# The head of an S5 stage: lag kernels in 16-row bands, C sums as a third PE term, 128-row transposes, identity matmuls between PE's steps

## The chip, the cores and the metric

The kernel runs on one core of one Trainium2 chip. The metric is the device time of one execution in microseconds (us), the median of several runs.

## The reference, cut to what matters

Input is x of 256 tokens by 1024 channels in fp32. Two blocks of two layers follow each other, eight stages in all: S5 mixer, SwiGLU, stick-breaking attention, SwiGLU, and twice a hybrid layer with its feed-forward part. The change touches the first stage alone, up to its gelu:

```python
bu_re = jnp.einsum('blgh,gph->lbgp', u, bb_re)
bu_im = jnp.einsum('blgh,gph->lbgp', u, bb_im)
_, _, s_re, s_im = lax.associative_scan(
    _ssm_combine, (a_seq_re, a_seq_im, bu_re, bu_im), axis=0)
y = (jnp.einsum('lbgp,ghp->blgh', s_re, c_re.astype(f32))
     - jnp.einsum('lbgp,ghp->blgh', s_im, c_im.astype(f32)))
y = y.reshape(bsz, seq, D_MODEL) + d_skip.astype(f32) * x.astype(f32)
h = jax.nn.gelu(y).astype(x.dtype)
val, gate = jnp.split(h @ w_glu, 2, axis=-1)
```

There are 64 groups of 16 channels, and 64 complex states in each group. The scan is linear with a constant factor (lambda) for each state.

## The kernel before

`s5_states` (from L186) computes that head. The main stream behind it multiplies with w_glu and all later weights; each of its matmuls is three fp32r products, wh by xTh, wh by xTl and wl by xTh (L783 to L785).

The head cuts the 256 tokens into 32 chunks (NC) of 8 tokens (TC). Two groups share the 128 partitions, so there are 32 pairs (NGP), in two halves f of 16. What happens inside a chunk is a table of lag kernels, 8 lags by 16 by 16 for each group; what happens between chunks is a short scan over 32 states. The steps have names, and one string, `ORDER`, sets the order in which they are written for TensorE, ScalarE, GpSimd and VectorE. SyncE's queue, which issues the DMAs, is ordered by the tile framework. The steps that matter here:

- L317 to L320: B and C are transposed in 32-column pieces (L252). Br and Bi are copied by ScalarE, their sum Bs is a GpSimd addition (L319).
- `ug`, `ut`, `us`: ScalarE gathers x into two tiles xTl and xTh (L406). TensorE transposes each in pieces of 32 rows, 64 transposes in all (L412). ScalarE stores u (L416).
- `cp`, `cs`: C times the discretisation factors (L446 to L452), giving cc0, cc1, cc2.
- `vp`, `vt`, `vs`: V, the input side, is B times powers of lambda, 24 VectorE products (L457) that read a table in PSUM (`lt`); 24 times four transposes on TensorE (L487); 24 copies (L491). `sm`, `sd`, `st`, `ss` make the chunk states of it (L500, L504, L509, L519).
- `wp`, `wq`: W, the output side, is C times powers of lambda by the three-product rule for complex numbers. GpSimd makes 24 products (L457 with LR, LRs and LRd); 16 sums (L468) on VectorE, some on GpSimd, combine them into a real and an imaginary half.
- `lp`, `lc`, `ld`: lag kernels. TensorE multiplies B with W (L598), ScalarE copies seven lags into `kz` (L602), VectorE adds the d_skip diagonal to the eighth (L605).
- `lw`: the shift. Eight DMAs for each of 4 quarters c and each half f, 64 in all and 64 KB each, copy windows of `kz` into `lagged` (L609), the band matrix that `tm` multiplies with u (L626). `kz` is one buffer for both halves, so the copies of f=1 overwrite what the DMAs of f=0 read.
- `mg`, `bo`: the scan between chunks on VectorE, up (three merges) and down (six border steps) for each half, four operations per step (L549 to L552).
- `om`: states times W into the same PSUM tiles (L633). `os` stores them (L638), `ot` transposes them back in pieces of 32 rows (L645), `og` is the gelu (L649), `oh` and `ol` split into the fp32r halves xTh and xTl (L652, L655).
- `wd`, `wh`, `wl` load and split the first w_glu tile early (L674 to L682); `hd` loads x again for the residual.

The main stream's weight loads (L737) use the pool `raws` with four buffers, and stand behind the shift DMAs in SyncE's queue.

Of the kernel before, what the change touches and what calls it, by code (L numbers as in the profile page):

```python
# [19 lines left out]
P = 128  # L20
# [145 lines left out]
ORDER = """
cp10 cp11 cs1 dk vp10 ug1 cp00 ug0 wp01 cp01 wp11 ut3 vp12 ut1 cs2 vt12 us3 ut0 vp01 vs12 cs0 wp21 vp11 wp31 us0 us1
vp02 vt10 vp00 vs10 vt01 vs01 vp31 ut4 vt11 wp22 wp02 wp30 vp30 wp00 ut2 vp22 vt02 vs11 wp20 us2 vt00 vs02 sm1 vt30
wq30 vp32 vs00 wp10 wq01 sm0 us4 vp21 vt22 sd1 vs30 dt wp12 wr1 st1 wq00 vs22 vt32 vp20 wq10 sd0 vt31 vp42 ds st0 vs32
wq11 vs31 ut7 ss0 wp32 wq21 vt20 vt21 wq31 wp70 ss1 vs20 sm3 wp50 dm vs21 wq20 wr0 vp41 sm2 wp40 sd3 sd2 wd vt42 lp0  # L170
bp0 ld01 vs42 vp51 vt41 ut5 lc00 wp71 ld00 lc01 lw00 vp50 wp51 vp52 vt51 wp61 wp42 st2 vs41 vt50 wp52 vp40 wq50 wp60
vs51 wp62 wp41 st3 wp72 lw03 ss2 vt40 vp70 us7 ut6 vs50 vs40 bt0 sm4 vp72 ss3 wq60 vt72 sd4 vp71 vs72 vt52 vs52 wh0
vt70 st4 bp1 vs70 wq51 lw01 vp62 us5 sm5 ss4 vp61 lw02 sd5 us6 vt61 bt1 wh1 vt71 wq70 vs71 vs61 vt62 vp60 wq40 st5
wq61 wq41 ss5 mg00 wq71 vt60 lp1 vs62 mg01 lc10 bp2 lc11 ld10 sm7 ld11 vs60 mg02 sd7 sm6 st7 wl1 bp3 bo00 sd6 ss7 bo01
bo02 st6 bo03 ss6 bo04 mg10 bo05 mg11 mg12 bo10 bo11 bo12 tm0 om0 os01 os00 bo13 lw13 lw10 ot1 ot2 og1 lw11 bo14 og2
oh11 ol11 ot3 oh21 ot0 lw12 ol21 oh10 og0 oh01 bo15 oh20 tm1 ol10 ol01 og3 om1 oh30 oh00 ol20 os11 wl0 os10 ot4 oh31
og4 oh40 ot7 ot6 hd ol00 og7 oh41 ol31 ol30 oh71 og6 ol40 oh70 ol41 ol70 oh61 ot5 og5 oh60 ol71 ol61 ol60 oh51 ol51
oh50 ol50
# [3 lines left out]
def s5_states(nc, tc, a, V, S, G, T, const, raws, ats, hpool, mm_ps, tp_ps, xts, ident, load_h, **_):  # L182
# [5 lines left out]
    nsm, nv = [0], [0]  # L188
# [22 lines left out]
    with tc.manual_schedule(engines=PAP):  # L211
# [103 lines left out]
        Br, Bi, Bs = (z.tile([P, NGP + (n != "Bs"), SH], F32, name=n) for n in ("Br", "Bi", "Bs"))  # L315
# [44 lines left out]
        squares, powers_at = [], []  # L360
# [32 lines left out]
        def ycol(ch):  # L393
            return first(("gel", ch), lambda: buf("gel", [P, SEQ]))
# [25 lines left out]
        for i in range(NK):  # L420
            step(f"ut{i}", u_transpose, i)
            step(f"us{i}", u_store, i)


        dsk, mask32, dmask = sm([P, 2, 8], "dsk"), sm([P, 32], "mask32"), sm([P, 2, 8, SH], "dmask")

        def skip_transpose():
            pd = tl["pd"] = tp_ps([P, 2 * 8])
            for c in range(4):
                T.matmul(pd[32 * c:32 * c + 32], d4[:, c, :], ident[:16, :16], start=True, stop=True)  # L430

        def skip_blocks():
            sh = [P, 2, 8, SH]
            G.tensor_mul(dmask, mask32[:, :SH].unsqueeze(1).unsqueeze(1).to_broadcast(sh), dsk.unsqueeze(3).to_broadcast(sh))

        step("dt", skip_transpose)
        step("ds", lambda: S.copy(dsk.rearrange("p f g -> p (f g)"), tl["pd"]))
        step("dk", lambda: V.tensor_reduce(mask32, ident.rearrange("p (c h) -> p h c", h=32), axis=AX.X, op=ALU.add))
# [22 lines left out]

        def w_product(i, k):
            dst = tmp(("wa", i), "wa", [P, 4, TC - 1, SH]) if k == 0 else W(k - 1)[:, 4 * i:4 * i + 4, :TC - 1, :]
            times(G, dst, cc[k], (LRr, LRs, LRd)[k], i, 1, TC - 1)

        def w_sum(i, k):
            w, e = W(k)[:, 4 * i:4 * i + 4, :TC - 1, :], (V, G)[i in POOL_SUMS]
            (e.tensor_add, e.tensor_sub)[k](w, w, tl["wa", i])  # L468

        for k in range(2):  # L470
            step(f"wr{k}", lambda k: S.copy(W(k)[:, :, TC - 1, :], cc[2 - k]), k)
        for i in range(8):
# [48 lines left out]

        def border_power(lv):

            L = sm([P, 3, NGP], f"L{lv}")
            lr, li = L[:, 0], L[:, 2]
            if lv == 0:
                V.tensor_copy(L[:, 0::2], LR[:, 0])
            else:
                pr, pi = squares[-1][:, 0], squares[-1][:, 2]
                V.tensor_mul(x1, pr, pr)  # L530
                V.tensor_mul(d2, pi, pi)
                V.tensor_sub(lr, x1, d2)
                V.scalar_tensor_tensor(li, pr, 2.0, pi, op0=ALU.mult, op1=ALU.mult)
            V.tensor_scalar(L[:, 1], li, -1.0, None, op0=ALU.mult)
            squares.append(L)
            powers_at.append(L)

        def border_table(lv):

            t = lt[1][:, 256 + 96 * lv:352 + 96 * lv].rearrange("p (i g) -> p i g", g=NGP)  # L540
            S.copy(t, powers_at[lv])
            powers_at[lv] = t

        def cmac(dst, x, lv, f, n, plus):
# [9 lines left out]
        def merge(f, lv):  # L554
            gs = slice(16 * f, 16 * f + 16)
            a0 = level(lv)[:, :, gs]
            cmac(level(lv + 1)[:, :, gs, :], a0[..., 0::2], lv, f, NC >> (lv + 1), a0[..., 1::2])

        def border(f, k):

            gs = slice(16 * f, 16 * f + 16)
            s, top = before()[:, :, gs], level(3)[:, :, gs]
            if k == 0:
                V.memset(s[..., 0:1], 0.0)
                V.tensor_copy(s[..., 8:9], top[..., 0:1])
            elif k < 3:
                cmac(s[..., 8 * k + 8:8 * k + 9], s[..., 8 * k:8 * k + 1], 3, f, 1, top[..., k:k + 1])
            else:
                lv = 5 - k
                st = 1 << lv  # L570
                cmac(s[..., st::2 * st], s[..., 0::2 * st], lv, f, NC >> (lv + 1), level(lv)[:, :, gs, 0::2])

        for lv in range(4):
            step(f"bp{lv}", border_power, lv)
        for lv in range(2):
            step(f"bt{lv}", border_table, lv)
        for f in range(2):
            for lv in range(3):
                step(f"mg{f}{lv}", merge, f, lv)
            for k in range(6):  # L580
                step(f"bo{f}{k}", border, f, k)
# [3 lines left out]
        kz = sm([P, 2 * TC - 1, 8, SH], "kz")  # L585
        G.memset(kz[:, TC:], 0.0)

        def by_parity(x, e):
            return x.rearrange("p t (q e) h -> p q e t h", e=2)[:, :, e]

        def lag_products(f):
            ks = tl["ks", f] = [mm_ps([P, 4, TC, SH]) for _ in range(G2)]
            for q in range(4):
                for k in range(2):
                    for c in range(4):
                        for e in range(G2):
                            gp, rows = 4 * (4 * f + c) + q, slice(64 * e, 64 * e + 64)
                            T.matmul(ks[e][32 * c:32 * c + 32, q], (Br, Bi)[k][rows, gp:gp + 2],  # L598
                                     W(k)[rows, gp].rearrange("p t h -> p (t h)"), start=(k == 0), stop=(k == 1))

        def lag_copy(f, e):
# [906 lines left out]
```

## Time and profile before

| what | value |
|---|---|
| median of 3 runs | 1380.1 us (1380.06 to 1381.06) |
| the profiled execution's own time | 1381.14 us |
| its span in the profile | 1379.2 us |
| TensorE busy | 1333.6 us, 97% of the span |
| VectorE busy | 915.7 us, 66% |
| ScalarE busy | 682.9 us, 50% |
| GpSimd busy | 86.3 us, 6% |
| mean granted TensorE clock | 0.986 |
| head, to the first matmul of the next projection (acc) | 129.1 us |

Times in a timeline or a chain are us from the start of the span. A group of equal instructions is one row with its count (x8). A busy time includes the pipeline's drain, so two rows that follow each other can overlap. "PEclk" is the clock that TensorE was granted, as a share of full speed.

### The profile page before, as it was taken

What the parts mean: (1) busy time and instruction counts of PE and PEld (TensorE: products, weight loads), DVE (VectorE), ACT (ScalarE), POOL (GpSimd) and SP (SyncE); (2) the same over time, 40 slices, a digit from 0 to 9 for tenths busy, and PEclk for the clock granted to TensorE, in tenths of its full rate; (3) what the DMA queues carried; (4) which work ended last, traced back from release to release, by engine and by line L of the source; (5) the groups of instructions that cost most, each with busy time, mean ns of one, the idle gap of its engine ahead of it and who ended that gap; (6) DMA issues with size and microseconds to landing.
All of it is one profiled execution on the core that took longest, in us unless ns stands there. A gap on an engine that the chain in (4) does not pass through costs nothing.

```text
span 1379.2 us, 20690 instructions
## 1 busy us (share of the span) xinstructions
PE 1333.6 (97%) x7439; PEld 1102.1 (80%) x7439; DVE 915.7 (66%) x1924; ACT 682.9 (50%) x1065; POOL 86.3 (6%) x153
## 2 busy tenths in 40 slices
PE   6769999999999999999999999999999999999998
PEld 5657878888888878888777888888887788888887
DVE  8677675555776775555888667555568866756462
ACT  3526444444587554444546545444455554545351
POOL 6400000000011100000200000000001000000000
PEclk9869999999999999999999999999999999999999
DMA  4359766556553475565364555564654535556561
GB/s 78 65 122 297 217 193 193 189 185 198 172 176 115 125 228 192 188 187 191 92 192 148 187 171 169 190 213 162 204 169 133 174 123 183 183 184 199 167 207 53
DMA packets 143398, 234.94 MB, mean 170 GB/s; under 512 B 16192, under 2 KB 84864, under 8 KB 143232
## 3 DMA queue, kind: packets, MB, share of 16 engines
q1 hardware_dynamic: 143296, 233.63, 54.5%
q8 instruction: 58, 0.95, 0.3%
q14 instruction: 44, 0.36, 0.1%
HBM read 228.35 MB, written 1.05 MB: 166 GB/s over the span
## 4 chain that ended last, share of the span: by engine, by line
PE 86%; DVE 5%; SPq 3%; DMA 2%; issue 1%; POOL 1%; ACT 1%; ACTq 0%; DVEq 0%; POOLq 0%
PE acc L784 8%; PE acc L785 8%; PE acc L783 8%; PE mm_ffn_g_t L784 5%; PE mm_ffn_g_t L785 5%; PE mm_ffn_g_t L783 5%; PE mm_ff_g_t L783 4%; PE mm_ff_g_t L785 4%; PE mm_ff_g_t L784 4%; SPq L609 3%; PE tp L842 2%; PE mm_hy_t L783 2%; PE mm_hy_t L785 2%; PE mm_hy_t L784 2%; DVE wl L746 1%
## 5 line engine op out<-in xcount | busy, mean ns | idle before, releaser
L746 DVE TENSOR_TENSOR wl<-raw,wh 128x512 fp32r<-128x512 f32 (+1 forms) x834 | 542.8, 686 | 147.2 <-ACT wh L740 136.1
L740 ACT CAST wh<-raw 128x1024 fp32r<-128x1024 f32 (+1 forms) x417 | 436.4, 1048 | 241.7 <-PE mm_ffn_g_t L784 36.5
L783 PE MATMUL acc<-wh,bTh 128*128 128x512 f32 x544 | 213.4, 392 | 0.0
L784 PE MATMUL acc<-wh,bTl 128*128 128x512 f32 x544 | 212.1, 390 | 0.4 <-DVE bTl L829 0.3
L785 PE MATMUL acc<-wl,bTh 128*128 128x512 f32 x544 | 212.3, 390 | 0.0
L783 PE MATMUL mm_ffn_g_t<-wh,xTh 128*128 128x512 f32 x352 | 140.6, 400 | 1.4 <-ACT xTh L828 1.4
L784 PE MATMUL mm_ffn_g_t<-wh,xTl 128*128 128x512 f32 x352 | 137.7, 391 | 0.4 <-DVE xTl L829 0.4
L785 PE MATMUL mm_ffn_g_t<-wl,xTh 128*128 128x512 f32 x352 | 137.6, 391 | 0.0
L829 DVE TENSOR_TENSOR bTl<-tp,bTh 128x256 fp32r<-128x256 f32 (+1 forms) x104 | 52.7, 513 | 124.2 <-ACT bTh L828 124.2
L784 PEld LDWEIGHTS acc<-wh,bTl 128*128 128x128 f32 x544 | 102.2, 188 | 21.9 <-DVE bTl L829 1.1
L828 ACT CAST bTh<-tp 128x256 fp32r<-128x256 f32 (+1 forms) x104 | 45.3, 443 | 149.2 <-PE tp L842 135.5
L785 PEld LDWEIGHTS acc<-wl,bTh 128*128 128x128 f32 x544 | 102.1, 188 | 21.3
L783 PEld LDWEIGHTS acc<-wh,bTh 128*128 128x128 f32 x544 | 102.2, 188 | 21.1 <-ACT bTh L828 0.3
L783 PE MATMUL mm_ff_g_t<-wh,xTh 128*128 128x512 f32 x256 | 102.7, 401 | 0.0
L785 PE MATMUL mm_ff_g_t<-wl,xTh 128*128 128x512 f32 x256 | 100.0, 391 | 0.0
L784 PE MATMUL mm_ff_g_t<-wh,xTl 128*128 128x512 f32 x256 | 99.7, 390 | 0.0
L783 PEld LDWEIGHTS mm_ffn_g_t<-wh,xTh 128*128 128x128 f32 x352 | 66.1, 188 | 14.4 <-ACT xTh L828 1.8
L784 PEld LDWEIGHTS mm_ffn_g_t<-wh,xTl 128*128 128x128 f32 x352 | 66.3, 188 | 13.8 <-DVE xTl L829 1.1
L785 PEld LDWEIGHTS mm_ffn_g_t<-wl,xTh 128*128 128x128 f32 x352 | 66.1, 188 | 13.8
L783 PE MATMUL mm_hy_t<-wh,xTh 128*128 128x512 f32 (+1 forms) x160 | 60.9, 381 | 0.8 <-DVE at L1289 0.6
L784 PE MATMUL mm_hy_t<-wh,xTl 128*128 128x512 f32 (+1 forms) x160 | 59.2, 370 | 1.5 <-DVE xTl L829 1.3
L785 PE MATMUL mm_hy_t<-wl,xTh 128*128 128x512 f32 (+1 forms) x160 | 59.2, 370 | 0.0
(458 smaller groups left out, 2037.2 us busy)
## 6 DMA issues: line engine op xcount, KB each, us to landing
raw<-in_w_ff_dram SPq DMA_DIRECT2D x128, 512.0 KB, 4.6
raw<-in_ffn_w_gu_dram SPq DMA_DIRECT2D x176, 256.0 KB, 4.2
raw<-in_w_in_dram SPq DMA_DIRECT2D x64, 512.0 KB, 4.1
raw<-in_ffn_w_down_dram SPq DMA_DIRECT2D x44, 512.0 KB, 4.6
raw<-in_ssm_w_glu_dram SPq DMA_DIRECT2D x32, 256.0 KB, 4.7
raw<-in_sb_w_qkv_dram SPq DMA_DIRECT2D x32, 256.0 KB, 4.2
raw<-in_w_out_dram SPq DMA_DIRECT2D x16, 512.0 KB, 4.3
raw<-in_ssm_w_out_dram SPq DMA_DIRECT2D x8, 512.0 KB, 5.0
```

The source lines that it names most:

```text
L609: nc.sync.dma_start(out=lagged(f)[SH * j:SH * j + SH, c].rearrange("p t g h -> p (t g h)"), in_=kz[32 * c:32 * c + SH, j:j + TC].rearrange ...
L740: S.copy(wh, raw)
L746: V.tensor_sub(l2[:, sl], r2[:, sl], h2[:, sl])
L783: T.matmul(ps, xh[:, k], wh, start=first, stop=False)
L784: T.matmul(ps, xl[:, k], wh, start=False, stop=False)
L785: T.matmul(ps, xh[:, k], wl, start=False, stop=last)
L828: S.copy(hi, ps)
L829: V.tensor_sub(lo, ps, hi)
L842: T.transpose(pt[:, k, :], src[:, k * P:(k + 1) * P], ident)
```

## The change

It touches the head alone.

- **Shift.** `kz` has 16-row bands, one for each quarter of the groups (n = 0 to 3, at partitions 32n), for both halves at once. Eight DMAs for each n write two quarters c each, 32 in all, and only the lags that are not zero. What stays zero in `lagged` is written before by four DMAs of 1 MB each (`lz`) from the zeroed `kz`.
- **C sums.** The `wq` sums are gone. The LR product stays as a tile `wd`, and TensorE adds it as a third term: in `lp` with Bd = Br - Bi (96 matmuls of a half where 64 stood, and 8 more for the diagonal), in `om` with `gap`, the difference of the states' halves (96 for 64). Bs is made on TensorE with 32 fp32 matmuls by the identity (`both`) and a ScalarE copy.
- **Transposes.** x takes 16 transposes of 128 rows instead of 64, the outputs 16 instead of 64; gelu, high and low halves run on 512 columns at once, 4 each.
- **Scan.** The first border steps run for both halves at once; the later ones apart as before.
- **Identity matmuls.** A name "=N" in `ORDER` writes N matmuls of the identity by 64 columns of it into columns 448 on of the PSUM tile `lt[1]`, whose other columns hold tables that VectorE reads.

```diff
-cp10 cp11 cs1 dk vp10 ug1 cp00 ug0 wp01 cp01 wp11 ut3 vp12 ut1 cs2 vt12 us3 ut0 vp01 vs12 cs0 wp21 vp11 wp31 us0 us1
...
+cp00 cp01 =12 dt ug0 =29 ut0 cp10 vp01 ds cp11 vt01 bm ug1 us00 us01 vp02 wd vs01 ut1 us10 =1 vt02 vp00 dk vp12 vs02
...
-        G.tensor_add(Bs, Br[:, :NGP], Bi[:, :NGP])
         Cc = [transposed(lambda hh: raw[:, hh, :], pv_ps) for raw in c_raw]
+        both = tp_ps([P, SH, NGP])
+        for hh in range(SH):
+            for i, raw in enumerate(b_raw):
+                T.matmul(both[:, hh, :], raw[:, :, hh], i32, start=(i == 0), stop=(i == 1))
+        S.copy(Bs, both.rearrange("p h g -> p g h"))
...
+        def u_transpose(n):
+
+            pu = tl["pu", n] = tp_ps([P, 4, 4, NC])
+            for k in range(4):
+                T.transpose(pu[:, k].rearrange("p r c -> p (r c)"),
+                            tl["xg", n // 2][:, 4 * (n % 2) + k].rearrange("c t h -> c (t h)"), ident)
...
-        def w_sum(i, k):
-            w, e = W(k)[:, 4 * i:4 * i + 4, :TC - 1, :], (V, G)[i in POOL_SUMS]
-            (e.tensor_add, e.tensor_sub)[k](w, w, tl["wa", i])
-
+        def columns(k, rows, gp):
+            return (wd if k == 2 else W(k))[rows, gp].rearrange("p t h -> p (t h)")
+
+        step("bm", lambda: G.tensor_sub(Bd, Br, Bi))
...
+        def lag_zeros(n):
+            nc.sync.dma_start(out=lagged(n // 2)[:, 2 * (n % 2):2 * (n % 2) + 2].rearrange("p c t g h -> p (c t g h)"),
+                              in_=kz.rearrange("p c t g h -> p (c t g h)"))
...
+        def lag_spread(n):
             for j in range(TC):
-                nc.sync.dma_start(out=lagged(f)[SH * j:SH * j + SH, c].rearrange("p t g h -> p (t g h)"),
-                                  in_=kz[32 * c:32 * c + SH, j:j + TC].rearrange("p t g h -> p (t g h)"))
...
+                nc.sync.dma_start(out=lagged(n // 2)[SH * j:SH * j + SH, 2 * (n % 2):2 * (n % 2) + 2, :TC - j].rearrange("p c t g h -> p c (t g h)"),
+                                  in_=kz[32 * n:32 * n + SH, :, j:].rearrange("p c t g h -> p c (t g h)"))
...
+        def state_outputs(f, k):
+            for gi, q, e in places:
+                gp, rows = 16 * f + 4 * q + gi, slice(64 * e, 64 * e + 64)
+                w = columns(k, rows, gp)
+                T.matmul(tl["pc", f][e][32 * q:32 * q + 32, gi, :w.shape[1]],
+                         gap[rows, gp - 16 * f, :] if k == 2 else before()[rows, k, gp, :], w, start=False, stop=(k == 2 and gi == 3))
...
             for name in ORDER.split():
-                steps.pop(name)()
+                if name[0] == "=":
+                    for _ in range(int(name[1:])):
+                        T.matmul(lt[1][:, 448:], ident, ident[:, :64], start=True, stop=True)
+                else:
+                    steps.pop(name)()
```

The order on two engines. TensorE, from the transposes of B and C to the first transposes of V; before:

```order
L252 MATMUL pv<-ident,c_136 128x32 x16
L412 MATMUL tp<-ident,xTl 128x32 x16
L487 MATMUL pv<-ident,v 128x128 x4
L412 MATMUL tp<-ident,xTh 128x32 x8
L487 MATMUL pv<-ident,v 128x128 x8
```

and with the change:

```order
L249 MATMUL pv<-ident,c_136 128x32 x16
L322 MATMUL tp<-ident,big_134 128x32 x32
L728 MATMUL lt_124<-ident 128x64 x12
L434 MATMUL tp<-ident,dpad 64x32 x2
L728 MATMUL lt_124<-ident 128x64 x29
L415 MATMUL tp<-ident,xTh 128x128 x4
L495 MATMUL pv<-ident,v 128x128 x4
L415 MATMUL tp<-ident,xTh 128x128 x4
```

32 matmuls for Bs and 41 identity matmuls (L728) now stand between the transposes of C and the first transposes of x.

TensorE, at the end of the head, with the change (`tp<-ident,raw` are the output transposes, `pv<-big_634` is `tm1`):

```order
L676 MATMUL tp<-ident,raw 128x128 x8
L728 MATMUL lt_124<-ident 128x64 x7
L822 MATMUL mm_s_g_t_1770<-wh,xTh 128x512
L651 MATMUL pv<-big_634,u 32x128 x32
L728 MATMUL lt_124<-ident 128x64
L664 MATMUL pv<-big_587,c_1238 32x128 x32
```

The first matmul of the main stream, which needs the high half of the first outputs, stands ahead of `tm1` and `om1`; before, it stood behind them.

SyncE's queue around the first main weight loads; before:

```order
L609 DMA big_1258<-kz 16x1024 x32
L150 DMA h<-in_x_dram 128x1024 x2
L737 DMA raw<-in_ssm_w_glu_dram 128x2x256 x8
L848 DMA lng<-in_ln_mix_g_dram 128x1024
```

and with the change:

```order
L150 DMA h<-in_x_dram 128x1024 [waits DMAHW4_49,DVE_49]
L150 DMA h<-in_x_dram 128x1024 [waits DMAHW5_49,DVE_49]
L887 DMA lng<-in_ln_mix_g_dram 128x1024 [waits DMAHW2_49,DMAHW1_49,DMAHW3_49,DMAHW0_49,DMAHW6_49,DVE_49,DMAHW7_49,PE_49,Pool_49]
L776 DMA raw<-in_ssm_w_glu_dram 128x2x256 [waits Activation_49]
L776 DMA raw<-in_ssm_w_glu_dram 128x2x256 [waits DVE_49,PE_49,Activation_49]
```

The load of `lng` has moved ahead of all main weight loads. It waits for TensorE (the last `om1` matmul), VectorE, GpSimd and the shift DMAs; the weight loads behind it wait with it, since a queue issues in order.

## Rows read from the trace of the kernel before

**Rows 1.** Windows of two stretches: length, busy (count) by engine, PEclk, DMA share, GB/s.

```profile
33.00:54.00 21.00, 17.95 (x387) 14.68 (x386) 16.82 (x27) 15.12 (x36) 17.60 (x17) 1.00 0.27 46
85.00:99.00 14.00, 9.32 (x224) 8.23 (x224) 6.97 (x18) 3.00 (x11) 0.00 (x0) 0.63 0.58 154
```

**Rows 2.** The chain of waits, 63 to 108 us: start, length, what.

```profile
63.90 2.35 DMA lag<-kz
66.35 0.98 ACT kz L602 x2
...
89.95 2.45 DMA big<-kz
92.44 3.63 PE mm L626 x56
96.07 3.16 PE mm L633 x128
99.25 0.69 DVE raw L638
...
102.01 5.19 DMA raw<-in_ssm_w_glu_dram
```

**Rows 3.** SyncE's queue, timeline: start, length, the issues as one row.

```profile
44.01 21.11 SPq L609 DMA_DIRECT2D lag<-kz  x32
67.61 22.93 SPq L609 DMA_DIRECT2D big<-kz  x32
...
91.69 14.27 SPq L737 DMA_DIRECT2D raw<-in_ssm_w_glu_dram  x8
```

**Rows 4.** TensorE, timeline of the head.

```profile
10.09 3.62 PE L252 MATMUL pv<-ident,c 32*128 32x32 f32 x32
...
23.65 1.97 PE L487 MATMUL pv<-ident,v 128*128 128x128 f32 x8
...
35.47 1.04 PE L487 MATMUL pv<-ident,v 128*128 128x128 f32 x8
36.35 0.38 PE L509 MATMUL mm<-ident,sls 128*128 128x128 f32 x2
...
47.03 1.08 PE L500 MATMUL mm<-vT,u 128*32 128x128 f32 x32
...
108.19 0.59 PE L783 MATMUL mm_s_g_t<-wh,xTh 128*128 128x512 f32 x1
...
129.14 0.39 PE L783 MATMUL acc<-wh,bTh 128*128 128x512 f32 x1
```

**Rows 5.** ScalarE, timeline of the head.

```profile
10.60 1.28 ACT L321 ACT_TABLE_LOAD   x1
...
15.80 0.39 ACT L355 ACTIVATE lt<-LR 128x256 f32<-128x256 f32 x1 [3.70 <-DVE LR L331]
...
17.46 1.06 ACT L406 COPY xTl<-big 128x1024 f32<-128x1024 f32 x1
```

**Rows 6.** GpSimd, groups by line and shape: count, busy us, mean ns, idle.

```profile
L457 POOL TENSOR_TENSOR wa<-cc,LR 128x448 f32<-128x448 f32 x8 | 9.6, 1218 | 1.0 <-DVE big L468 1.0
L457 POOL TENSOR_TENSOR big<-cc,LRd 128x448 f32<-128x448 f32 x8 | 9.0, 1144 | 0.0
L457 POOL TENSOR_TENSOR big<-cc,LRs 128x448 f32<-128x448 f32 x8 | 8.1, 1039 | 6.3 <-DVE cc L451 6.3
```

**Rows 7.** VectorE, timeline: steps of the scan between chunks.

```profile
57.96 0.42 DVE L549 TENSOR_TENSOR mt<-h,lt 128x256 f32<-128x256 f32 x1
...
59.42 0.18 DVE L530 TENSOR_TENSOR sm<-L 128x32 f32<-128x32 f32 x1
...
72.82 0.62 DVE L549 TENSOR_TENSOR mt<-c,lt 128x256 f32<-128x256 f32 x1
...
75.11 0.69 DVE L549 TENSOR_TENSOR mt<-c,lt 128x512 f32<-128x512 f32 x1
...
77.75 0.69 DVE L549 TENSOR_TENSOR mt<-c,lt 128x512 f32<-128x512 f32 x1
```

More of the change, by code (lines that the diff above doesn't have):

```diff
@@ L175 @@
[L175 to L178, printed above, removed]
+cp00 cp01 =12 dt ug0 =29 ut0 cp10 vp01 ds cp11 vt01 bm ug1 us00 us01 vp02 wd vs01 ut1 us10 =1 vt02 vp00 dk vp12 vs02
+vp10 cs2 vp11 vt00 ut2 vs00 bp0 vt12 vp22 dm vp20 us11 vs12 vt10 sm0 vt11 vp21 vs10 us20 wp12 vt22 sd0 vs11 vp30 ut3
@@ L179 @@
+sm6 mg00 sm7 sd6 wl0 st6 sd7 lw0 mg01 =4 st7 ss6 wp50 ss7 wp52 =5 lp1 mg02 lc310 mg10 lc300 mg11 lc301 lc311 lc200 lw3
+lc201 mg12 lc211 bo0 bo1 bo2 bo3 lc210 =40 tm0 bo04 bo05 =12 om00 =1 om01 bo14 lw2 sx0 =1 om02 hd bo15 os01 os00 =12
+ot01 ot00 sx1 og00 og01 oh01 =7 tm1 =1 om10 =1 om11 =1 om12 oh00 os10 os11 =8 ot11 og11 ot10 ol01 ol00 og10 oh10 oh11
+ol10 ol11
 """
@@ L418, in s5_states, with u_store @@
+        def u_store(n, f):
+            S.copy(u[f].rearrange("p (r k) c -> p k r c", r=2)[:, 4 * n:4 * n + 4], tl["pu", n][:, :, 2 * f:2 * f + 2])
         for i in range(2):
             step(f"ug{i}", u_gather, i)
[L420 to L425, printed above, removed]
+        for n in range(4):
+            step(f"ut{n}", u_transpose, n)
+            for f in range(2):
+                step(f"us{n}{f}", u_store, n, f)
@@ L570, in border @@
                 st = 1 << lv
[L571 to L576, printed above, removed]
+                cmac(s[..., st::2 * st], s[..., 0::2 * st], lv, gs, NC >> (lv + 1), level(lv)[:, :, gs, 0::2])
+        step("bp0", border_first)
+        for lv in range(3):
+            if lv < 2:
+                step(f"bt{lv}", border_table, lv)
+            step(f"bp{lv + 1}", border_power, lv + 1)
         for f in range(2):
@@ L579, in s5_states @@
                 step(f"mg{f}{lv}", merge, f, lv)
[L580 to L589, printed above, removed]
+            for k in (4, 5):
+                step(f"bo{f}{k}", border, slice(16 * f, 16 * f + 16), k)
+        step("bo0", border_top)
+        for k in (1, 2, 3):
+            step(f"bo{k}", border, slice(0, NGP), k)
@@ L591, in lag_products @@
+        kz = sm([P, 2, TC, 8, SH], "kz")
+        G.memset(kz, 0.0)
+        def lag_zeros(n):
+            nc.sync.dma_start(out=lagged(n // 2)[:, 2 * (n % 2):2 * (n % 2) + 2].rearrange("p c t g h -> p (c t g h)"),
+                              in_=kz.rearrange("p c t g h -> p (c t g h)"))
         def lag_products(f):
             ks = tl["ks", f] = [mm_ps([P, 4, TC, SH]) for _ in range(G2)]
+            at = [(c, e, slice(64 * e, 64 * e + 64)) for c in range(4) for e in range(G2)]
             for q in range(4):
[L594 to L599, printed above, removed]
@@ L612, in s5_states @@
-        for f in range(2):
-            step(f"lp{f}", lag_products, f)
-            for e in range(G2):
-                step(f"lc{f}{e}", lag_copy, f, e)
-                step(f"ld{f}{e}", lag_diagonal, f, e)
-            for c in range(4):
-                step(f"lw{f}{c}", lag_spread, f, c)
+                for k in range(3):
+                    for c, e, rows in at:
+                        gp = 4 * (4 * f + c) + q
+                        w = columns(k, rows, gp)
+                        T.matmul(ks[e][32 * c:32 * c + 32, q].rearrange("p t h -> p (t h)")[:, :w.shape[1]],
+                                 (Br, Bi, Bd)[k][rows, gp:gp + 2], w, start=(q == 0 and k == 0), stop=False)
@@ L627, in lag_outputs @@
                          start=(gi == 0), stop=False)
-        def state_outputs(f):
-            for k in range(2):
-                for gi, q, e in places:
-                    gp, rows = 16 * f + 4 * q + gi, slice(64 * e, 64 * e + 64)
-                    T.matmul(tl["pc", f][e][32 * q:32 * q + 32, gi, :], before()[rows, k, gp, :],
-                             W(k)[rows, gp].rearrange("p t h -> p (t h)"), start=False, stop=(k == 1 and gi == 3))
+        gap = z.tile([P, 16, NC], F32, name="gap")
```

189 lines of the change are left out of this document (101 added, 88 removed).

## The prediction

> **What bounds the kernel now.** I read the page first (TensorE is busy for 97% of the span, so it can only win where it idles), then the slices, the windows, the chain of waits, SyncE's queue, and the engines' timelines over the head. Two stretches of the head show it. From 33 to 54 us TensorE works 17.95 of 21 us at full clock; from 85 to 99 us it works 9.32 of 14 us at a mean granted clock of 0.63, that is, mostly at the lower of its two levels (1.2 and 2.4 GHz) [rows 1]. Between them the chain of waits leaves the computing engines: SyncE issues 32 shift DMAs in 21.11 us, the last one lands at 66.25, only then may ScalarE overwrite `kz`, and SyncE issues 32 more in 22.93 us [rows 2, 3]. Only when the last of these has landed, at 92.4, can `tm1` go on (3.63 us) and `om1` follow (3.16 us); its last matmul is done at 99.2 [rows 2]. I call this moment E. The main weight loads stand behind the shift DMAs in the queue (issued from 91.69, 14.27 us for eight), and so TensorE's steady work begins at 108.19, nine us after E, and the next projection at 129.14 [rows 3, 4]. From there on both kernels have the same matmuls in the same order. So the change is worth what it does to E, and to the stretch from E to the steady work.
>
> **What the shift costs now.** Each half has 16 DMAs instead of 32. At 21.11/32 = 0.66 us per issue [rows 3] that is 10.6 us, and with bands of its own for each n, `kz` need not wait for the first half's landing. The second half can be issued as soon as `lp1` and its copies are done (below, 60 us): 60 + 1 + 10.6 + 2.45 = 74 us, where `tm1` stands at 81. So the shift leaves the path, with 7 us to spare, and both its halves of 21 and 23 us with it. The four zero fills, 4.2 MB together, are issued from 15 to 35 us on; at the 154 GB/s of [rows 1] they take 27 us and are done before the first shift DMA at about 50, so I cost them at nothing. What covers them is the stretch in which W and V are made; without it the 27 us would stand ahead of the shift. What is late next is VectorE's scan, and ahead of it a head that now begins later.
>
> **The start, later by about 5 us, then 5 more.** The 32 matmuls for Bs stand behind the transposes of C, which end at 10.09 + 3.62 = 13.7 [rows 4]. One of these records takes 3.62/32 = 0.113 us. The new ones are fp32 matmuls of the same shape: one record each gives 3.6 us, two records 7.2. I take 5.7, since the fp32 matmuls of L500 show two records each (16 matmuls stand there, x32 in [rows 4]) and some can overlap; 19.4 us. ScalarE copies Bs behind them (0.6), loads its table (1.28), scales and copies three tables (0.39 each) and only then gathers x (1.06) [rows 5], an extra 4.5 with the warm-up: the first gather ends near 23.5, where it ended at 18.5.
>
> The 41 identity matmuls ahead of `ut0` write the same PSUM tile as the table that ScalarE scales at about 21.9, and wait for it. No row shows one; the nearest are 128-column transposes, eight in 1.97 us at the lower level and eight in 35.47 to 36.35 = 0.88 at the higher [rows 4], so 0.11 to 0.24 each, 4.5 to 9.6 us for 41. I take 5, nearer the higher level, as they have half the columns: `ut0` at 26.9. In return I expect the transposes behind them at the higher level, where those at 23.65 still ran at the lower one.
>
> **From there to the first merge, TensorE's own work.** 24 x 4 transposes of V and 4 x 4 of x at 0.44 make 28 x 0.44 = 12.3 us; six `sm` at 1.08 [rows 4] 6.5; five `st` at 0.22 1.1; `lp0`, 96 matmuls or 192 records, by half of 3.16 us per 128 [rows 2] 2.4; 25 identity matmuls at 0.11 2.8. That is 25.1, with half a us of waits `mg00` begins at 52.5. The 48 transposes saved in x (64 became 16) are in this sum.
>
> GpSimd runs beside it: 24 products in 9.6 + 9.0 + 8.1 = 26.7 us [rows 6], without its sums and additions. They start later, since the V product `vp00` ahead of the cc2 they need reads the PSUM tile that the identity matmuls write, and so waits for the one behind `ut1`: near 31, done near 57. `lp1` then is near 60, off the path by 15 us.
>
> **VectorE's scan.** A level-0 step takes 77.75 - 75.11 = 2.64 us, level 1 upwards 59.42 - 57.96 = 1.46, level 1 downwards 75.11 - 72.82 = 2.29 [rows 7], level 2 about 1.0 (estimate, from half of 1.46 and the fixed part). Up, both halves: 2 x (2.64 + 1.46 + 1.0) = 10.2. Down to the first `gap`: bo0 to bo3 for both halves 0.3 + 0.8 + 0.8 + 2.3, then 2.29 + 2.64, then the other half's 2.29 and the subtraction 0.6: 12.0. With 1.1 us for three waits on identity matmuls, which share the tile, that ends at 75.8.
>
> **The tail to E.** `om02` 0.8, two stores 1.2 on ScalarE, eight output transposes 0.9, two gelus 1.2, the high half 0.6, one main matmul 0.24: 80.7. Then `tm1` and the 96 matmuls of `om1`: half of 3.63 and 1.5 x half of 3.16 are 4.2 at the higher level, with their waits 4.8, twice 4.2 at the lower [rows 2]. So E lies between 85.5 and 90; I take 87, since the 40 identity matmuls ahead of `tm0` and 12 behind `om0` keep TensorE going through most of its waits. Before: 99.2. **Minus 12.2 us.**
>
> **From E to the steady work.** The load of `lng` is now ahead of the weight loads, and waits for E. Then: its issue 0.4, the f=0 low halves that free a buffer for the weights 2.1, two issues 0.9, a landing of 5.19 [rows 2], the cast 1.05: E + 9.6, against E + 9.0 before. TensorE waits some 5 us of it and may then begin at the lower level, as it did before: the matmul at 108.19 took 0.59 us, the one at 129.14 0.39 [rows 4]. I add 2. **Plus 2.5 us** in this stretch.
>
> **Sum.** -12.2 + 2.5 = -9.7 on the profiled execution's 1381.1 (span 1379.2), which is 1.0 over the median of 1380.1. 1371.4; against the median it would be 1370.4. **I forecast 1371.**
>
> **Rivals.**
>
> *The clock stays low through TensorE's stretch (slower).* Transposes are 112 of the matmuls between 27 and 52 us. If TensorE ran that stretch at its lower level, each of 28 groups of four would take 0.95 instead of 0.44: 28 x 0.51 = 14.3 more, `mg00` at 67, E at 101, and the end at 1381.1 - 9.7 + 14.3 = 1385.7. It decides from 9.7/0.51 = 19 groups on. For it: the eight transposes at 23.65 took 1.97 us, with TensorE at work around them [rows 4]. Against it: from 33 to 54 us, with transposes for much of its work, the granted clock stayed at 1.00 [rows 1]. 0.11. The Trainium skill, "TensorE: Matmul & The Clock Gate", section "Part 4: PE-mode transpose", has the rule for this: the raised clock "doesn't engage" for transposes, which don't count as busy in the same way. By that page the time would be this rival's; the trace bears it out at 23.65 us, not at 35.47.
>
> *The identity matmuls are slow.* At 0.24 each ahead of `ut0`, and the clock no higher for them: +4.6, 1376. For it: the transposes that stand there now ran at the lower level [rows 4]. 0.20.
>
> *All ends low.* One record for each Bs matmul (-2.1), `tm1` and `om1` at the higher level (-1.5) and no loss of clock behind E (-2): 1381.1 - 15.3 = 1366. 0.14.
>
> *The transfers stay on the path.* The change halves the number of transfers, but the bytes that are moved rise from 4.2 to about 6.5 MB with the zero fills; if the bytes set the pace, or `lw2`'s copies come late behind the merges, `tm1` waits again near 92 and E is where it was: 1380. Against it: DMA engines were 0.58 busy in [rows 1] with 64 KB transfers, and the fills run early. 0.10.
>
> **How the numbers follow.** The forecast has 0.45, the rivals as given. A measurement of this kernel can tell about 0.2% from no change, 2.8 us: faster is below 1377.3. Faster: 0.45 + 0.14 + 0.20, less a little for the rival at 1376 that reaches over the bound: 0.77. Same: the transfers' rival and that little: 0.12. Slower: the clock's: 0.11. The range 1364 to 1381 reaches over the fast end and the transfers' rival, and leaves out the clock's and some 0.08 below and above.
>
> **What would show it.** The shift DMAs in two stretches of some 10 us, and `tm1` not released by a DMA; `ut0` near 27 us; `mg00` near 52; the scan 23 us long without a gap; E near 87; the first weights' cast some 9 us behind E; full clock in 1-us windows from 27 to 52. Wrong: transposes of 0.95 us per four in that stretch, a landing ahead of `tm1`, or TensorE's steady work beginning more than 10 us behind E.

## The result, and the profile after

The change makes the kernel slower: 1417.22 us (1415.74 to 1419.55, 4 runs) against 1380.08 of the kernel before, a ratio of 1.0269 (95% interval 1.0252 to 1.0287). The profiled execution took 1417.67 us, its span is 1415.9. The first matmul of the next projection stands at 164.21 us where it stood at 129.14 [rows 4], so 35.1 of the 36.7 us that the span grew by lie in the head, as the prediction placed them. Their sign is the other one. One execution in this document, of experiment 7, took 2857 us; it counts in no interval.

TensorE in the changed kernel, columns as in [rows 4]; L322 are the matmuls for Bs, L728 the identity matmuls, L415 the transposes of x, L664 `om`:

```profile
14.95 14.03 PE L322 MATMUL tp<-ident,big 32*128 32x32 f32 x64
31.45 5.39 PE L728 MATMUL lt<-ident 128*128 128x64 f32 x24 [2.46 <-ACT lt L358]
...
37.12 12.63 PE L728 MATMUL lt<-ident 128*128 128x64 f32 x58
49.55 1.06 PE L415 MATMUL tp<-ident,xTh 128*128 128x128 f32 x4
...
91.56 9.14 PE L728 MATMUL lt<-ident 128*128 128x64 f32 x80 [0.72 <-DVE mt L564]
100.64 2.03 PE L651 MATMUL mm<-lag,u 128*32 128x128 f32 x64
104.28 3.71 PE L728 MATMUL lt<-ident 128*128 128x64 f32 x24 [1.61 <-DVE mt L564]
107.92 1.96 PE L664 MATMUL mm<-big,c 64*32 64x128 f32 x64
...
131.16 0.43 PE L664 MATMUL pv<-wd,gap 64*32 64x112 f32 x16 [0.21 <-issue]
...
142.30 0.79 PE L822 MATMUL mm_s_g_t<-wh,xTh 128*128 128x512 f32 x1 [5.38 <-ACT wh L779]
```

Bs takes 14.0 us. The first 12 identity matmuls are 24 records and the next 29 are 58: each is two records of 0.218 us, 18 us for the 41. At 91.56, 80 records take 9.14, 0.114 each. So one identity matmul costs 0.44 us at TensorE's lower clock level and 0.23 at the higher. The moment E, the end of the last `om1` product, is 131.6 instead of 99.2, and steady work begins at 142.3. In TensorE's groups up to 145 us the identity matmuls are the largest:

```profile
L728 PE MATMUL lt<-ident 128*128 128x64 f32 x318 | 51.6, 333 | 6.3 <-DVE mt L564 3.8 <-ACT lt L358 2.5
```

On ScalarE the copy of Bs (L323), the table load, the tables and the gather of x (L409) stand behind those matmuls in that order, where the gather stood at 17.46 [rows 5]:

```profile
29.02 0.59 ACT L323 COPY raw<-tp 128x512 f32<-128x512 f32 x1 [17.02 <-PE tp L322]
29.62 1.28 ACT L324 ACT_TABLE_LOAD   x1
...
31.03 0.37 ACT L358 ACTIVATE lt<-LR 128x256 f32<-128x256 f32 x1
...
31.86 1.06 ACT L409 COPY xTh<-big 128x1024 f32<-128x1024 f32 x1
```

VectorE waits for identity matmuls, because they write the tile that holds its tables. These four rows are the first V product that needs the tile again (L461) and three steps of the scan (L563); in brackets is the idle time before and what ended it:

```profile
52.21 0.69 DVE L461 TENSOR_TENSOR v<-raw,lt 128x512 f32<-128x512 f32 x1 [18.33 <-PE lt L728]
...
81.62 0.70 DVE L563 TENSOR_TENSOR lt<-c,lt 128x512 f32<-128x512 f32 x1 [1.46 <-PE lt L728]
...
100.75 0.64 DVE L563 TENSOR_TENSOR lt<-c,lt 128x256 f32<-128x256 f32 x1 [3.05 <-PE lt L728]
...
110.53 0.63 DVE L563 TENSOR_TENSOR lt<-c,lt 128x256 f32<-128x256 f32 x1 [4.97 <-PE lt L728]
```

The shift itself does what was forecast. SyncE's queue, answering to [rows 3]; the third row is the main weight loads behind E:

```profile
77.00 12.44 SPq L633 DMA_DIRECT2D lag<-kz  x16
93.14 12.05 SPq L633 DMA_DIRECT2D big<-kz  x16
...
132.14 6.57 SPq L776 DMA_DIRECT2D raw<-in_ssm_w_glu_dram  x8
```

Two stretches of 12 us replace 21 and 23, and the row of `tm0` above follows directly on identity matmuls, not on a transfer.

My theory after this: the identity matmuls and the 32 matmuls for Bs lie on the path and cost nearly four times and two and a half times what I allowed; bands, third term and 128-row transposes are a gain. The rivals: the identity matmuls pay for a part by holding the clock up, or the rest of the change is no gain either.

### The profile page after: what moved, and what is told of

The parts are those of the page before. It is cut to its first block, busy times and chain, and to the rows that moved or that the text cites. A ratio compares the mean times of both kernels' runs of the same rounds, so it can differ in the third digit from the quotient of the medians.

```text
span 1415.9 us, 21753 instructions
## 1 busy us (share of the span) xinstructions
PE 1382.7 (98%) x8009; PEld 1155.0 (82%) x8009; DVE 905.5 (64%) x1881; ACT 688.2 (49%) x1065; POOL 80.3 (6%) x149
## 4 chain that ended last, share of the span: by engine, by line
PE 91%; DVE 5%; DMA 1%; ACT 1%; issue 1%; POOL 0%; SPq 0%; ACTq 0%; DVEq 0%; POOLq 0%
PE acc L824 8%; PE acc L823 8%; PE acc L822 8%; PE mm_ffn_g_t L823 5%; PE mm_ffn_g_t L824 5%; PE mm_ffn_g_t L822 5%; PE mm_ff_g_t L822 4%; PE mm_ff_g_t L824 4%; PE mm_ff_g_t L823 4%; PE lt L728 3%; PE tp L881 2%; PE mm_hy_t L823 2%; PE mm_hy_t L822 2%; PE mm_hy_t L824 2%; PE mm_s_g_t L822 1%; PE mm_hy_b_t L824 1%
## 5 line engine op out<-in xcount | busy, mean ns | idle before, releaser
L823 PE MATMUL mm_hy_t<-wh,xTl 128*128 128x512 f32 (+1 forms) x160 | 59.8, 374 | 1.5 <-DVE xTl L868 1.3
L824 PE MATMUL mm_hy_t<-wl,xTh 128*128 128x512 f32 (+1 forms) x160 | 59.8, 374 | 0.0
```

Of the source, the lines that this page charges most:

```text
L823: T.matmul(ps, xl[:, k], wh, start=False, stop=False)
L824: T.matmul(ps, xh[:, k], wl, start=False, stop=last)
```

## The experiments

Each was run beside the kernel before on the same chip.

**1. No identity matmuls.**

```diff
-                    for _ in range(int(name[1:])):
+                    for _ in range(0):
```

> All identity matmuls are left out, nothing else. Theory P (they are paid for in full: each is two records of 0.22 us at the lower clock, 0.11 at the higher): the first x transposes begin as soon as the gather allows, at 33 us where they began at 49.6; 25 identity matmuls fewer (5.7 us) before the first merge; the scan loses its waits of 3.0 and 5.0 us; the end of the head's last product (E) near 100 us instead of 131.6, 1386 us in all (1380 to 1392). Rival C (they hold TensorE's clock up and so pay for a good part): everything behind them runs at the lower clock, 20 to 25 us of the gain go back, 1405 us or more.

Measured: 1384.82 us, 1.0036 of the kernel before (1.0019 to 1.0053). 32 us are gone. The first x transposes of this kernel wait for the gather alone, and nothing but transposes runs for the next six us:

```profile
32.97 1.12 PE L415 MATMUL tp<-ident,xTh 128*128 128x128 f32 x4 [3.61 <-ACT xTh L409]
...
35.58 1.92 PE L495 MATMUL pv<-ident,v 128*128 128x128 f32 x8
37.29 1.06 PE L415 MATMUL tp<-ident,xTl 128*128 128x128 f32 x4
38.14 1.29 PE L495 MATMUL pv<-ident,v 128*128 128x128 f32 x8
...
40.38 1.09 PE L495 MATMUL pv<-ident,v 128*128 128x128 f32 x8
```

Eight transposes take 1.92 us, then 1.29, then 1.09: the clock rose near 38.6, with only transposes at work. Rival C falls in its size: it wanted 1405 us or more, and the total lies at theory P's 1386. In a small part it is right, as `tm0` shows, which took 2.03 us behind 40 identity matmuls in the changed kernel and runs at the lower level without them:

```profile
77.78 3.66 PE L651 MATMUL mm<-lag,u 128*32 128x128 f32 x64 [5.56 <-DMA lag<-kz]
```

It also waits for a shift transfer here. That wait is not the one that counts: `om0`, behind it, waits another 1.95 us for VectorE's scan.

**2. Bs by GpSimd, identity matmuls kept.**

```diff
-        both = tp_ps([P, SH, NGP])
-        for hh in range(SH):
-            for i, raw in enumerate(b_raw):
-                T.matmul(both[:, hh, :], raw[:, :, hh], i32, start=(i == 0), stop=(i == 1))
-        S.copy(Bs, both.rearrange("p h g -> p g h"))
+        G.tensor_add(Bs, Br[:, :NGP], Bi[:, :NGP])
```

> Bs is again GpSimd's addition; the 32 matmuls by the identity and the copy are gone; the other identity matmuls stay. Theory P: those 32 took 14.0 us on the path and the table load waits behind the copy, so all that follows moves up by 14 us: 1403 us (1400 to 1406). Rival: ScalarE's table scaling, which waits for VectorE's powers (done at 16.9 us), or the x gather is late anyway: less than 8 us gained, 1409 or more.

Measured: 1411.76 us (1403.93 to 1413.44), 1.0215 (1.0183 to 1.0248). By its total the run lies on the rival's side (1409 or more). In its profiled execution, the one of 1403.93, the x transposes begin 13.5 us earlier, at 36.03, and the granted clock is at its higher level from 92 to 113 us; the three others have a lower mean clock (0.986 to 0.989 against 0.996) and take 1410 us and more. So in the profiled execution the 13.5 us are there, against the rival's reason. Up to 10 us come and go with the clock; that the three others lost it in the late stretch of identity matmuls, as the changed kernel does, is not shown, since no trace of them was kept.

**3. Both edits.**

> Both edits: no identity matmuls, Bs by GpSimd. What is left of the change is bands, third term and 128-row transposes. Theory P: the two prices add: 1386 - 14 = 1372 us (1366 to 1378), faster than the kernel before by about 8 us, and the shift DMAs are not waited for. Rival S (the rest of the change is itself no gain, since GpSimd and the scan on VectorE set E): 1380 us or more.

Measured: 1374.17 us (1373.69 to 1375.82), 0.9953 (0.9935 to 0.9971). The prices nearly add: 1384.8 less the 14 us of Bs is 1371, and what came off is 10.7 us. TensorE, with `tm0`, `om0`, the last of `om1` and the steady work:

```profile
63.84 3.66 PE L647 MATMUL mm<-lag,u 128*32 128x128 f32 x64 [4.98 <-ACT kz L624]
70.20 2.99 PE L660 MATMUL mm<-big,c 64*32 64x128 f32 x128 [2.69 <-DVE c L562]
...
88.88 0.76 PE L660 MATMUL pv<-wd,gap 64*32 64x112 f32 x35 [1.44 <-issue]
...
100.46 0.80 PE L818 MATMUL mm_s_g_t<-wh,xTh 128*128 128x512 f32 x1 [6.04 <-ACT wh L775]
```

`om0` is released by VectorE's scan: that is the bound in place of the shift. E is 89.6, the steady work E + 10.8. VectorE ahead of the first merge (L559) shows a wait for TensorE's lag products and a low half (L713) that takes 3.37 us, where the next one takes 0.68. It ends half a us behind GpSimd's last product (the last row):

```profile
44.42 0.69 DVE L457 TENSOR_TENSOR v<-Bi,lt 128x512 f32<-128x512 f32 x1 [4.01 <-PE pv L491]
45.97 3.37 DVE L713 TENSOR_TENSOR wl<-raw,wh 128x512 fp32r<-128x512 f32 x1 [0.87 <-PE pv L491]
...
49.89 0.69 DVE L559 TENSOR_TENSOR lt<-c,lt 128x512 f32<-128x512 f32 x1
```

```profile
47.81 0.98 POOL L457 TENSOR_TENSOR big<-cc,LRd 128x448 f32<-128x448 f32 x1
```

**4. Only the 41 ahead of the x transposes left out** (`=12` and `=29` taken out of `ORDER`).

> Only the 41 identity matmuls ahead of the first x transposes are left out; Bs stays on TensorE, the other 117 stay. If each group is paid for where it stands: the x transposes begin at 33 us instead of 49.6, and all behind moves up by 16 to 17 us: 1400 us (1396 to 1404). If those 41 pay by raising the clock for the transposes behind them: a part comes back, 1405 or more.

Measured: 1401.93 us (1397.47 to 1407.01, at mean clocks from 0.997 to 0.989), 1.0143 (1.0113 to 1.0172). By the medians the 41 cost 15 us, the other 118 the 17 that remain to experiment 1; with these executions the split is good to some 5 us.

**5. A tile of their own.**

```diff
+                    dm = tp_ps([P, 64])
                     for _ in range(int(name[1:])):
-                        T.matmul(lt[1][:, 448:], ident, ident[:, :64], start=True, stop=True)
+                        T.matmul(dm, ident, ident[:, :64], start=True, stop=True)
```

> All identity matmuls stay where they are, but write a PSUM tile of their own instead of the columns beside VectorE's tables. VectorE no longer waits for them (18.3, 3.0 and 5.0 us in the change's trace), nor they for VectorE. If the shared tile is a cost of its own, V and W are ready earlier and the scan loses 8 us of waits: 1408 us (1403 to 1412). If TensorE's in-order stream alone sets the time, the waits of VectorE only move: 1414 to 1418.

Measured: 1406.15 us (1405.55 to 1406.54), 1.0173 (1.0156 to 1.0190). 11 us of the 37 go with the shared tile. 3.0 of them are won up to `tm0` (97.67 us instead of 100.64), where VectorE's waits for identity matmuls are gone. The other 8.4 lie between `tm0` and E, and there the clock differs. Windows over `om0`, the output transposes and the identity matmuls around them, columns as in [rows 1], first of the changed kernel:

```profile
104.00:125.00 21.00, 20.27 (x272) 18.32 (x276) 7.33 (x13) 3.30 (x6) 0.00 (x0) 0.59 0.25 63
```

and of this one:

```profile
98.00:119.00 21.00, 20.31 (x573) 17.82 (x565) 7.19 (x13) 3.30 (x6) 0.00 (x0) 1.00 0.40 81
```

TensorE is as busy in both, 20.3 of 21 us, and does twice as many matmuls in the second. The four executions have mean clocks of 0.996 and 0.997, those of the changed kernel 0.990 to 0.994. Why the clock falls with the shared tile is not shown. The wait ahead of the 12 identity matmuls is not enough: in the profile of experiment 2 the tile is shared, TensorE waits there as long as in the changed kernel (1.62 us against 1.61), and the same 24 records run at the higher level, 2.89 us where they took 3.71:

```profile
93.80 2.89 PE L724 MATMUL lt<-ident 128*128 128x64 f32 x24 [1.62 <-DVE mt L560]
```

**6. What sets the price.** Two runs of one execution each, with other forms for the first 12 and the next 29 (1406.72 and 1404.89 us).

```diff
...
+                        if name == "=12" and "vt00" in steps:
+                            T.matmul(lt[1][:32, 448:], ident[:, :32], ident[:, :64], start=True, stop=True)
+                        elif name == "=29":
+                            T.matmul(lt[1][:, 448:464], ident, ident[:, :16], start=True, stop=True)
+                        elif name == "=18":
+                            T.transpose(lt[1][:, 448:], ident[:64], ident[:64, :64])
...
```

> What sets the price of an identity matmul. The first 12 have a stationary operand of 32 columns instead of 128, the next 29 a moving operand of 16 columns instead of 64, the 18 behind the first lag products are transposes of 64 rows; the others stay. If the stationary operand's load sets it, the 12 take a quarter to a half of 0.44 us each, the 29 still 0.44, and the transposes, one record each, 0.11 instead of 0.23 at the higher clock. If the moving columns set it, the 12 stay at 0.44 and the 29 fall to 0.11 to 0.2. If a fixed cost sets it, all stay at two records of 0.22.

TensorE, the 12, the 29 and the 18:

```profile
31.47 2.77 PE L729 MATMUL lt<-ident 128*32 128x64 f32 x24 [2.47 <-ACT lt L358]
...
34.52 9.46 PE L731 MATMUL lt<-ident 128*128 128x16 f32 x58
...
70.63 1.34 PE L733 MATMUL lt<-ident 64*128 64x64 f32 x18
```

A quarter of the stationary columns halves a record (0.218 to 0.113), a quarter of the moving ones takes a quarter off (0.16), and none of the three theories holds alone; the transposes are one record of 0.07 us each, at the higher level, where a record of the same 128 stationary and 64 moving columns took 0.114. The second run has both operands small for the 12, and fp32r for the 29:

```diff
...
+                            T.matmul(lt[1][:32, 448:464], ident[:, :32], ident[:, :16], start=True, stop=True)
...
+                            T.matmul(lt[1][:, 448:], neg_gt, neg_gt[:, :64], start=True, stop=True)
...
```

> The price again. The first 12 have a stationary operand of 32 columns and a moving one of 16, the next 29 are fp32r matmuls of a triangle of ones by its first 64 columns, the rest as in the change. In e5_price a quarter of the stationary columns halved the price and a quarter of the moving ones took a quarter off it. If both loads add, the 12 take 0.11 us each (two records of 0.055). If fp32 costs two records because it is passed twice, the fp32r ones are one record each and the 29 take 0.22 or less instead of 0.44 at the lower clock.

```profile
31.44 1.47 PE L729 MATMUL lt<-ident 128*32 128x16 f32 x24 [2.47 <-ACT lt L358]
...
33.19 6.40 PE L731 MATMUL lt<-neg_gt 128*128 128x64 f32 x29
```

Both as expected: 24 records in 1.4 us, 0.058 each, and one record instead of two for fp32r, 0.214. Per column, stationary and moving cost about the same in these five forms, 0.0011 to 0.0012 us at the lower level, one behind the other; fp32 pays it twice. It is no rule for others: the matmuls for Bs, with 128 stationary and 32 moving columns, would take 0.18 us a record by it and took 0.22.

**7. Identity matmuls in waits alone.** Experiment 3 with 66 of them, 40 ahead of `tm0`, 12 ahead of `om0`, 14 in the tail, in a tile of their own.

> Bs by GpSimd and no identity matmuls up to the second lag products, as in e3_neither; behind that 66 of them stand in TensorE's waits (40 ahead of tm0, 12 ahead of om0, 14 in the tail) and write a tile of their own. If they can keep the clock up where TensorE waits anyway: tm0 falls from 3.7 to 2.0 us, om0 from 5.0 to 3.4, tm1 from 3.5 to 2.0, om1 a little: 1370 us, 4 below e3_neither. If they cost as much as they bring: within 2 us of e3_neither (1374), or above it.

Measured: 1378.44 us, 0.9977 (0.9962 to 0.9993), some 3 us more than experiment 3. The 40 took 9.1 us from 59.8 on, which puts `tm0` at 68.8 instead of 63.8 us, and with the 12 behind it `om0` at 73.6 instead of 70.2. They did keep the clock up, and what they saved by it they had cost before:

```profile
59.77 9.14 PE L725 MATMUL tp<-ident 128*128 128x64 f32 x80
68.84 2.03 PE L647 MATMUL mm<-lag,u 128*32 128x128 f32 x64
```

`tm0` fell from 3.66 to 2.03 us and `om0` from 5.8, with a stop in it, to 2.8, as hoped; `om0` ends at 76.5, in experiment 3 at 76.0. `tm1` stayed near the lower level, 3.11 us.

**8. The weight loads ahead of `lng`.** Experiment 3 with the gelu results in `kz`.

```diff
-            return first(("gel", f), lambda: raws.tile([P, 4, NC, TC], F32, name="raw", tag="raw"))
+            return kz[:, f].rearrange("p t g h -> p (t g h)").rearrange("p (q c j) -> p q c j", q=4, j=TC)
```

> e3_neither with the two gelu results in kz (free by then) instead of two of the four raw buffers. The main weight loads then stand ahead of lng in SyncE's queue and find free buffers at about 76 us instead of 91. If the loads behind lng are what TensorE waits for at 94 to 100 us, the first weights are cast right behind E and steady work begins at about E + 4 instead of E + 11: 1368 us (1365 to 1371). If the casts' own buffers, which take the head's memory, set it, no change: 1374.

Measured: 1370.26 us, 0.9912 (0.9897 to 0.9926). SyncE's queue:

```profile
76.40 15.82 SPq L772 DMA_DIRECT2D raw<-in_ssm_w_glu_dram  x8
93.96 0.34 SPq L883 DMA_DIRECT2D lng<-in_ln_mix_g_dram  x1
```

The loads now precede `lng`; the next projection begins at 116.4 us against 122.4 in experiment 3. The size is two thirds of what I expected; the eight issues still stretch over 15.8 us, where they take 6.6 behind E in the changed kernel.

**9. VectorE's path shortened, then a few identity matmuls.** The low halves of the early weights behind the third merge, on top of experiment 8; and that with 16 identity matmuls ahead of `tm0` and 10 ahead of `om0`, in a tile of their own.

> e7_gelu_kz with the two low halves of the early weights moved on VectorE to behind the third merge of the first half. In e3_neither the first of them took 3.4 us instead of 0.6, beside GpSimd's last products, just ahead of the first merge. If the scan sets the end of the head, it begins 3 us earlier, and what is left after the wait for the second half's states is 1.7 us: 1368.5 us (1367 to 1370). If E hangs on TensorE's tail alone: 1370, no change.

Measured: 1369.26 us, 0.9907 (0.9888 to 0.9925): 1 us, inside its interval. The low half was not the cause of its 3 us. With it gone, the next operation of VectorE takes them, a step that needs 0.18 us elsewhere; it ends at 48.9, as GpSimd's last product does (48.8), and the first merge begins at 49.33:

```profile
44.90 3.98 DVE L536 TENSOR_TENSOR sm<-L 128x32 f32<-128x32 f32 x1
```

> e8_wl_late with 26 identity matmuls in a tile of their own, 16 ahead of tm0 and 10 ahead of om0, sized by their measured price of 0.23 us at the higher clock to fit in TensorE's waits (3.7 us and 2.3 us). If they can be free where they fit and keep the clock up: tm1 (3.2 us) and the output transposes fall to the higher clock's times, 2 us: 1366.5. If they are no gain even so: 1368 to 1370.

Measured: 1368.52 us (1366.03 to 1375.90), 0.9895 (0.9870 to 0.9919). Not told apart from the one without them. The version of experiment 8, or the first of 9, is the one to keep: 11 to 13 us under the kernel before.

**10. The shift in 64 transfers again,** bands and bytes as in experiment 3.

```diff
-                nc.sync.dma_start(out=lagged(n // 2)[SH * j:SH * j + SH, 2 * (n % 2):2 * (n % 2) + 2, :TC - j].rearrange("p c t g h -> p c (t g h)"),
-                                  in_=kz[32 * n:32 * n + SH, :, j:].rearrange("p c t g h -> p c (t g h)"))
+                for c in range(2):
+                    nc.sync.dma_start(out=lagged(n // 2)[SH * j:SH * j + SH, 2 * (n % 2) + c, :TC - j].rearrange("p t g h -> p (t g h)"),
+                                      in_=kz[32 * n:32 * n + SH, c, j:].rearrange("p t g h -> p (t g h)"))
```

> e3_neither with each shift DMA split in two by quarter, so that 64 are issued again instead of 32, for the same bytes; bands and zero fills stay. At 0.78 us each (12.4 to 13.2 us for 16) the first half lands near 77 us instead of 64 and the second near 103. If the halved count is what takes the shift off the path: om0 waits until 81 and om1 until 107, 1374 + 14 = 1388 us (1382 to 1392). If the bytes set the pace and not the number: 1374 to 1376.

Measured: 1388.44 us, 1.0050 (1.0033 to 1.0068), 14 above experiment 3. SyncE's queue and TensorE's `tm0` and `tm1`:

```profile
47.18 22.70 SPq L630 DMA_DIRECT2D lag<-kz  x32
69.98 22.07 SPq L630 DMA_DIRECT2D big<-kz  x32
```

```profile
70.75 3.98 PE L648 MATMUL mm<-lag,u 128*32 128x128 f32 x64 [12.15 <-DMA lag<-kz]
...
92.65 3.91 PE L648 MATMUL pv<-big,u 128*32 128x128 f32 x64 [7.98 <-DMA big<-kz]
```

For the same bytes, the number of issues decides: `tm0` and `tm1` wait for transfers again. (With 0.70 us an issue, not 0.78, the two halves landed some 6 and 10 us earlier than I had written; that the total agrees all the same is in part luck.) The run also shows what halving carries: with 64 issues the kernel is 7 us slower than the one before. So the 7 us that experiment 3 gains are the 14 of the halved issues, less 7 for the rest of the change together; the third term and the larger transposes were not priced alone.

## Why the prediction was wrong

The way to E in four legs, forecast, measured in the changed kernel, and in experiment 3; the third column is the forecast without the terms that experiment 3 leaves out (8.4 us of the start, 2.8 and 1.1 us):

| leg | forecast | changed kernel | forecast without them | experiment 3 |
|---|---|---|---|---|
| to the first x transpose | 26.9 | 49.6 | 18.5 | 20.2 |
| to the first merge | 25.6 | 32.1 | 22.8 | 29.7 |
| the scan, to `gap` | 23.3 | 31.6 | 22.2 | 22.9 |
| the tail, to E | 11.2 | 18.4 | 11.2 | 16.8 |
| E | 87 | 131.6 | 74.7 | 89.6 |

**The step that failed** is "The start, later by about 5 us, then 5 more", in two terms, and one mechanism that it left out.

- *The 32 matmuls for Bs*, "I take 5.7": 14.0. My upper bound, two records of 0.113, took the record of a transpose. The trace had two records for an fp32 matmul, which I used, but no plain fp32 matmul with 128 stationary columns. Two records it was, but of 0.219 us each. Experiment 6 shows the same at other columns: a transpose's record is the cheaper one, 0.07 against 0.114 for 128 stationary and 64 moving columns. The sum by columns gives only 0.18 for Bs, so the rest of its price stays open.
- *The 41 identity matmuls*, "0.11 to 0.24 each, 4.5 to 9.6 us ... I take 5": 0.44 each, 18.0. Here I forgot the second record altogether, though the step above used it, and the value that I took supposed the higher clock. Experiments 1 and 4 price them at some 15 us for these and 17 for the rest. The rival "The identity matmuls are slow" had the place and the sign of the error, but my bound for its price.
- *The waits of VectorE*, "1.1 us for three waits on identity matmuls": the scan takes 31.6 us from 81.6 to 113.2, where I wrote 23.3; in experiment 3, without them, 22.9. Experiment 5 puts the shared tile at 11 us in all, the clock included.
- *The clock*, "In return I expect the transposes behind them at the higher level", "keep TensorE going through most of its waits": the first failed, the second held in part. 18 us of identity matmuls ran at 0.218 us a record from first to last (the PEclk column reads 1.00 there, and also from 20 to 33 us in the kernel before, where [rows 4] has transposes at the lower level; the durations say otherwise), and the clock rose near 51.5 us, behind the first transposes: four took 1.06 us at 49.55 and 0.75 at 51.25. The 40 ahead of `tm0` kept it (2.03 us for `tm0`, 3.66 without them). Behind `tm0` it fell, 0.59 over 21 us, though TensorE was busy for 20.3 of them, so `om0` took 1.96 us for 64 records and not the 1.16 that the same 64 take in experiment 5.

A second, smaller error shows only in the last two columns. That experiment 3 ends at 1374, near my 1371, is not my sum: without the identity matmuls and Bs on TensorE it gives 1359. 6.9 us are missing in the second leg, where I let TensorE's work run without a wait: `lp0` takes 4.2 us (39.6 to 43.8, with a stop of 1 us in it) for my 2.4, and the first transposes run at the lower clock. Nor does GpSimd only run "beside it": one of VectorE's last operations ahead of the first merge stretches until GpSimd's 24 products are done, 3.4 us in experiment 3, 3.98 in experiment 9, and 5.09 in the changed kernel (74.44 to 79.53, GpSimd's last product ending at 78.97). Why VectorE is held was not tried. And 5.6 us are missing in the tail, where I had taken the higher clock for most of it: `tm1` is 3.46 us for my 1.8, and TensorE stops in `om0` and `om1` for 1.19 and 1.44 us.

**What held.** The shift off the path: two stretches of 12 us (forecast 10.6; an issue is 0.75 to 0.78 us, not 0.66, and 0.83 in experiment 3), no transfer ahead of `tm0` in the changed kernel, and worth 14 us by experiment 10. The scan as next bound, 22.9 us against 23.3. The zero fills cost nothing that can be seen. The sign of the change without its two terms is as forecast: experiment 3 is 7.2 us under the kernel before.

**What came out right by luck.** From E to the next projection it is 2.7 us more than before (32.6 against 29.9), forecast 2.5, but the terms are not the ones forecast. The 108.19 of [rows 4] is not where TensorE's steady work began in the kernel before; the clock rose there. The work runs without a wait from this row on, 5.0 us behind E:

```profile
104.18 0.80 PE L783 MATMUL mm_s_g_t<-wh,xTh 128*128 128x512 f32 x1
```

In the changed kernel it begins 10.7 us behind E, 5.7 later and not 0.6. The 2 us for a low clock are no difference, since the lower level lasts to about 108.6 before and from 142.3 to 147.1 now. In return 12 of the stage's 96 matmuls are done ahead of the wait, where 3 stood ahead of 104.18, and the rest takes 3.1 us less.

The rival of a low clock over transposes falls: in experiment 1 the clock rose with nothing but transposes at work. The Trainium skill's rule that the raised clock doesn't engage for them ("TensorE: Matmul & The Clock Gate", "Part 4: PE-mode transpose") is not what these rows show: the clock rose between eight transposes of 1.92 us and eight of 1.09.

## What to carry to other kernels

Price an added matmul from a row of its own kind: data type, stationary columns and moving columns together; a transpose's row says nothing about an fp32 matmul. Filler that TensorE works off in order is paid for where it does not fit into a wait, and again where its tile is one that another engine uses; no run here shows a gain by it. 159 fillers cost 32 us, 66 placed in waits some 3, and 26 that nearly fit were worth nothing measurable. Where a queue issues many small transfers, count the issues: halving them was the gain, and it showed once the filler was gone. When an operation of one engine takes many times what its like takes, look at what the others do until it ends: moving it away moved the time to the next one.

## What the runs showed that I had not expected

- Filler that keeps TensorE busy did not raise its clock, but it could hold it. At the lower level, 82 identity records (18 us) left it there, while six us of transposes raised it in experiment 1. At the higher level, 80 in a row (9.1 us) kept it, in the changed kernel and in experiment 7.
- The same kernel's executions differ by up to 10 us with the clock, where there are late fillers (experiment 2, 1403.9 to 1413.4 us, mean clock 0.996 to 0.986; experiment 4, 1397.5 to 1407.0, 0.997 to 0.989). In experiment 3, without any, they lie within 2.2 us; in experiment 1, also without any, within 7.4 (mean clock 0.993 to 0.986), so the filler is not the whole of it.
- Inside `om1`, TensorE stands still for 0.8 to 3.3 us in seven of these traces for nothing that the profile names (1.44 "issue" in experiment 3's row; none in experiment 1). What it waits for was not tried.
